# Experts in program order on TensorE, last w2 loads ahead of the norm loads, modulation rows spread by matmul, and pool places released tile by tile

## Chip, cores and metric

The kernel runs on one core of a Trainium2 chip (one TensorE, VectorE, ScalarE, GpSimd and SyncE with their own instruction queues, and 16 DMA engines). The metric is the device time of one execution in microseconds; the median of three runs counts.

## What is computed

One transformer block on 512 latent rows of 1024 channels, with 256 context rows beside them. Token mixing (latent attention and differential attention, gated, then one output projection) ends in a first norm; a mixture of 16 experts follows, of which each takes the 64 rows that score highest for it. The change lies in the second half, which is this, cut from the reference:

```python
y = gates[..., :D] * (o_mla @ w_o_mla) + gates[..., D:] * (o_diff @ w_o_diff)   # gated merge
o_lat = y @ w_out
x = layer_norm(ALPHA * x + g1 * o_lat, ln1_g, ln1_b)
h = x * (1.0 + sc2) + sh2
aff = softmax(h @ w_router + b_router)            # 16 experts
g, idx = lax.top_k(swapaxes(aff, 1, 2), 64)       # 64 rows per expert
xe = h[bidx, idx]
hid = silu(xe @ w1) * (xe @ w3)
ye = (hid @ w2) * g
x = layer_norm(ALPHA * x + g2 * zeros.at[bidx, idx].add(ye), ln2_g, ln2_b)
```

g1, sh2, sc2 and g2 are rows of 1024 modulation values, made out of c early in the kernel. Each expert's w1, w3 and w2 are 1024 x 1024 float32 (4 MB each, 201 MB in all), and each is read once.

## The kernel before

The program is written for a layer that records instructions, gives each tile a place in a pool, draws the waits, and lets a scheduler choose the order on each engine from modelled costs; the order is fixed when the program is built, and each engine then works through its own list. A pool that is opened on bytes of closed pools waits, as written, for every user of those pools.

**Merge, output projection, router.** For each of eight channel blocks of the latent branch (tile `om`, helper lines 82 to 84: a float32 product out of three passes of 128x512) VectorE gates it (line 902), GpSimd adds the other branch (line 904, `ys`), and ScalarE and VectorE split it into `yh`, `yl`. The gates are one tile `th` of 16 slices. The output projection (tile `po`) runs over two column halves of four token tiles, 24 matmuls each. g1 scales its result: in the first half afterwards (line 1007), in the second half beforehand, by multiplying the raw weights `outraw` on GpSimd (line 888), which are then split into `woh` and `wol` on ScalarE and VectorE (lines 75 and 78). For this g1 is needed on all 128 partitions (`g1b`); GpSimd's partition_broadcast makes it out of the row tile `rm` (line 968), and likewise `g2b` later (line 1187). After each `po` tile come four transposes, the router's products and, in the second half, the norm and the affinities; VectorE then finds the 64 largest.

**Experts in pairs.** For each of eight pairs: `gather` picks the rows by one-hot matmuls (line 1102, 32 matmuls of 128x128, into PSUM tiles `mx`; VectorE writes `xe`), `up_` does w1 and w3 of one expert (line 1140, `h`, 32 matmuls on 64 array columns each, two side by side), `back` transposes the one-hots (line 1120), `hid_t` transposes the hidden rows (line 1151), `down` does w2 (line 1159, `y`), and `scatter` scales, splits (`ye`) and puts the rows back: per column half four `mx` tiles of two matmuls (line 1171), each added to the accumulators by VectorE (line 1172). The last pair's `down` goes by three column parts (384, 384, 256 wide, line 1265), each put back while the next is computed (lines 1240 to 1254); then comes the second norm.

**Loads.** SyncE's queue issues nearly all of them in order (lines 934 and 936 for the experts). A load of 512 KB (384 KB in the first two parts of the last pair) fills one of 36 ring places of four pools, or one of nine places of tiles that are needed later (`places`: `gb`, `ye`, `acc0` to `acc3`, `hid`, `ohT`, `hidT`). A load waits until its place's last reader is done. A piece of weights is loaded when the program first asks for it, or earlier when `prefetch` is called. The gains and biases of the last norm (line 1222, `ln`) go into the places of `xe` and `hid`, which the last pair's `up_` and `hid_t` read, and are written ahead of the code that asks for most of the last w2 pieces.

Of the kernel before, what the change touches and what calls it, by code (L numbers as in the profile page):

```python
# [10 lines left out]
F32 = mybir.dt.float32  # L11
# [41 lines left out]
def _layer(tc, A, out, opened):  # L53
# [32 lines left out]
    # ---------------------------------------------------------------- constants and small vectors  # L86
# [12 lines left out]
    ghv = cp.tile([128, KD], F32, name="ghv")       # routed input = ghv * normed + bhv  # L99
# [21 lines left out]
    # ---------------------------------------------------------------- modulated input, first projection  # L121
# [10 lines left out]
    dqs = [rB.tile([128, NT, 256], F32, name="dq", tag="dq", bufs=2) for _ in range(2)]      # two heads each  # L132
# [92 lines left out]
    def mod_mul(q):  # L225
        """scale and shift of 256 channels, as rows"""
# [21 lines left out]
    def x_chunk(k, ci):  # L248
        """128 channels of the latent (0) or context (1) rows: transposed, modulated, split"""
# [16 lines left out]
    for q in range(4):  # L266
        # beside the products of these channels: what makes the next
# [15 lines left out]
    # rotary tables: cos, signed sin for the keys; the query ones carry the score scale  # L283
# [42 lines left out]
    one32 = mw.tile([128, 32], F32, name="one32")  # L326
    V.memset(one32, 1.0)
# [20 lines left out]
    def mod_sum(j, wa):  # L348
# [3 lines left out]
        for g in (2 * h, 2 * h + 1):  # L352
            T.matmul(pm[32 * g:32 * g + 32, :], one32, wa[:, (g % 2) * 512:(g % 2) * 512 + 512], start=True, stop=True)
# [3 lines left out]
    def chunk(col, n, cuts, evac, at, nxt):  # L357
        """projected columns; after the tiles in `at`, a part of the modulation's rows"""
# [27 lines left out]
    # latent query and key ranks: rms norm, transpose, gain  # L386
# [55 lines left out]
    def gates(g4, at=()):  # L442
        """a quarter of the gates, transposed: weights stationary"""
# [10 lines left out]
        for j in range(4):  # L454
            S.activation(th[:, g4 * 4 + j, :], ac[j], AF.Tanh, scale=0.5)
# [40 lines left out]
    # score tiles are emitted one by one; between them goes the product work of the tiles before  # L496
# [13 lines left out]
    def fill(parts):  # L510
        """one score tile is out: emit one of `parts` equal shares of the waiting work"""
# [12 lines left out]
    def flush(key=None):  # L524
        """emit all the waiting work, or what has `key`"""
# [7 lines left out]
    # transposed queries and keys: even heads of the differential attention, then the latent ones | odd heads  # L533
# [21 lines left out]
    def prep_t(hd, m, nm, src, c0, t0, nn):  # L555
# [8 lines left out]
        if nm == "q1":  # L564
            # the same with the halves of the contraction swapped
# [13 lines left out]
    def mod_end():  # L579
# [13 lines left out]
        # router columns with the norm's gain, less their mean: the norm's own mean then drops out  # L593
# [33 lines left out]
    # ---------------------------------------------------------------- differential attention  # L627
# [23 lines left out]
    def transposed(ws_, wt, j):  # L651
        """key chunks 2j, 2j+1 of two [128 q, 768] tiles, into [128 keys, 6, 256 q]"""
# [11 lines left out]
    def finish(hd, av, z0, key):  # L664
# [5 lines left out]
        def norm():  # L670
# [3 lines left out]
            # rows are scaled by the first map's sum: so is the guard under the root  # L674
# [23 lines left out]
    def key_rows():  # L698
        """the rotated key part, on rows 64-96 of every head's keys"""
# [35 lines left out]
    for hd in range(DH):  # L735
# [3 lines left out]
        for half in range(2):  # L739
# [6 lines left out]
            for t in (2 * half, 2 * half + 1):  # L746
# [9 lines left out]
                # sum0 * (softmax0 - lam * softmax1) = e0 + e1 * (-lam * sum0 / sum1)  # L756
# [24 lines left out]
    # ---------------------------------------------------------------- latent attention  # L781
# [16 lines left out]
    def diff_out(c, hl, jj):  # L798
# [4 lines left out]
        V.scalar_tensor_tensor(th[:, KD + j, :], th[:, KD + j, :], 1.0, ps, op0=OP.add, op1=OP.mult)  # L803

    for h in range(HEADS):
# [4 lines left out]
        for half in range(2):  # L810
# [52 lines left out]
    # ---------------------------------------------------------------- gated merge  # L863
# [14 lines left out]
    def w_out_load(hf, kk, page_):  # L878
        """two contraction chunks of a column half of w_out"""
# [15 lines left out]
    for c in range(4):  # L895
        hl = wos[c]
        for jj in range(2):
# [4 lines left out]
            V.scalar_tensor_tensor(g, th[:, j, :], 1.0, ps, op0=OP.add, op1=OP.mult)  # L902
            ys = yt.tile([128, 512], F32, name="ys")
            G.tensor_tensor(ys, g, th[:, KD + j, :], op=OP.add)
# [6 lines left out]
    # ---------------------------------------------------------------- expert weights: pages filled ahead  # L911
# [426 lines left out]
```

## Time and profile before

| what | value |
|---|---|
| runs | 1096.82, 1097.37, 1098.73 us (median 1097.37) |
| span of the profiled execution | 1094.2 us, first to last instruction |
| median of the runs less that span | 3.2 us |
| TensorE busy | 1007.4 us (92%) |
| weight loads on TensorE | 630.1 us |
| VectorE, ScalarE, GpSimd busy | 454.8, 276.0, 204.4 us |
| mean granted TensorE clock | 0.976 |
| DMA | 266.97 MB, mean 244 GB/s |

The profiled execution is known by its span alone; the runs' times have 3.2 us around it. In the profile PE is TensorE's matmuls, PEld its weight loads, DVE VectorE, ACT ScalarE, POOL GpSimd, SPq SyncE's queue of transfers. A float32 matmul appears as two records (so 4 records of `h` are one 512 KB page of weights), a float32r pass as one. The ends of matmuls are modelled and records overlap, so that a group's time over its count says more than the length of one. "idle before <- X" is what ended the wait.

### The profile page before, as it was taken

The page shows a single profiled execution, that of the slowest core. Times are in us where ns is not written, and L with a number is a line of the kernel's source. Part 1 is how long each engine was busy: PE and PEld are TensorE (multiplying, and loading weights), DVE is VectorE, ACT ScalarE, POOL GpSimd, SP SyncE. Part 2 cuts the span into 40 slices and gives each one's busy share as a digit, 9 for nine tenths or more (in the row PEclk, how much of TensorE's full clock was granted, in tenths as well). Part 3 has the DMA queues.
Part 4 walks back from the last instruction along what each step waited for, and adds up shares of the span by engine and source line. Part 5 has one row for each costly group of instructions (what it writes and reads, how often), then busy time and mean ns, then how long its engine had stood idle before and what let it go on. Part 6 is the DMA issues. An engine that isn't in the chain of part 4 may idle for free.

```text
span 1094.2 us, 13748 instructions
## 1 busy us (share of the span) xinstructions
PE 1007.4 (92%) x5259; PEld 630.1 (58%) x5259; DVE 454.8 (42%) x832; ACT 276.0 (25%) x551; POOL 204.4 (19%) x193
## 2 busy tenths in 40 slices
PE   6999998998899999997849999999999999999972
PEld 5888977677787777675536634444434434343331
DVE  2372377643677466463584221303022131303127
ACT  1222325244677455431210101010101010100001
POOL 2340022021675222143214200000000000000004
PEclk9999999999899999999889999999999999999997
DMA  9943357741002000176678999999999999999082
GB/s 302 288 154 106 97 169 247 243 140 39 20 20 74 20 20 21 39 269 235 245 270 304 404 329 411 409 409 409 409 409 409 409 410 408 409 410 400 14 283 97
DMA packets 101209, 266.97 MB, mean 244 GB/s; under 512 B 14020, under 2 KB 37528, under 8 KB 101144
## 3 DMA queue, kind: packets, MB, share of 16 engines
q1 hardware_dynamic: 100248, 264.52, 65.8%
q0 software_dynamic: 320, 1.05, 0.3%
q8 instruction: 41, 0.67, 0.3%
q10 hardware_dynamic: 576, 0.52, 0.1%
q14 instruction: 24, 0.20, 0.1%
HBM read 261.47 MB, written 2.10 MB: 241 GB/s over the span
## 4 chain that ended last, share of the span: by engine, by line
PE 75%; DVE 9%; DMA 5%; ACT 4%; issue 3%; POOL 2%; SPq 0%; DVEq 0%; ACTq 0%; POOLq 0%
PE h L1140 22%; PE y L1159 9%; PE mx L1102 6%; PE acc L84 4%; PE acc L83 4%; PE sc L648 4%; PE acc L82 4%; PE mx L1171 3%; PE tpb L656 3%; PE av L836 2%; DMA wa<-w_ada 2%; DMA wraw<-w_in 2%; PE y L1265 1%; PE av L772 1%; PE tp L232 1%
## 5 line engine op out<-in xcount | busy, mean ns | idle before, releaser
L1140 PE MATMUL h<-wr,xe 128*64 128x512 f32 x1024 | 250.0, 601 | 0.0
L1140 PEld LDWEIGHTS h<-wr,xe 128*64 128x64 f32 x1024 | 76.0, 136 | 110.4 <-issue 94.5
L1159 PE MATMUL y<-wr,hidT 128*64 128x512 f32 x448 | 99.6, 595 | 0.7 <-ACT hidT L1152 0.7
L1146 DVE TENSOR_TENSOR hid<-hid,h 128x512 f32<-128x512 f32 x16 | 11.0, 687 | 203.6 <-PE h L1140 203.6
L1102 PEld LDWEIGHTS mx<-oh,xn 128*128 128x128 f32 x512 | 62.7, 195 | 39.9 <-issue 38.7
L637 DVE TENSOR_REDUCE nm<-sc 128x1 f32<-128x768 f32 x64 | 61.0, 954 | 38.7 <-PE sc L648 38.2
L1115 POOL TENSOR_TENSOR oh<-oh,aff 128x512 f32<-128x512 f32 x8 | 8.4, 1049 | 361.9 <-PE mx L1102 353.1
L1102 PE MATMUL mx<-oh,xn 128*128 128x128 f32 x512 | 72.6, 289 | 1.7 <-DVE oh L1094 1.7
L1159 PEld LDWEIGHTS y<-wr,hidT 128*64 128x64 f32 x448 | 34.0, 137 | 57.8 <-issue 53.2
L638 ACT ACTIVATE P<-sc,nm 128x768 f32<-128x768 f32 x64 | 57.6, 900 | 35.0 <-DVE nm L637 26.0
L1145 ACT ACTIVATE hid<-h 128x512 f32<-128x512 f32 x16 | 9.6, 597 | 195.1 <-PE h L1140 195.1
L75 ACT ACTIVATE whi<-wraw 128x1024 fp32r<-128x1024 f32 (+1 forms) x32 | 33.5, 1046 | 99.6 <-DMA wraw<-w_in 80.9
L78 DVE TENSOR_TENSOR wlo<-wraw,whi 128x1024 fp32r<-128x1024 f32 (+1 forms) x32 | 38.7, 1211 | 43.9 <-PE acc L83 28.7
L82 PE MATMUL acc<-xlh,whi 128*128 128x512 f32 x128 | 51.0, 398 | 3.6 <-ACT whi L75 2.2
L82 PE MATMUL acc<-whi,xlh 128*128 128x512 f32 (+1 forms) x128 | 49.5, 391 | 1.0 <-ACT whi L75 1.0
L83 PE MATMUL acc<-xll,whi 128*128 128x512 f32 x128 | 50.0, 391 | 0.0
L84 PE MATMUL acc<-xlh,wlo 128*128 128x512 f32 x128 | 49.4, 394 | 0.3 <-DVE wlo L78 0.3
L84 PE MATMUL acc<-whi,xll 128*128 128x512 f32 (+1 forms) x128 | 48.8, 382 | 0.5 <-POOL xll L78 0.5
L83 PE MATMUL acc<-wlo,xlh 128*128 128x512 f32 (+1 forms) x128 | 48.8, 381 | 0.2 <-DVE wlo L78 0.2
L1172 DVE TENSOR_TENSOR acc<-acc,mx 128x512 f32<-128x512 f32 x56 | 36.0, 684 | 30.0 <-PE mx L1171 30.0
L648 PE MATMUL sc<-K,Q 96*128 96x512 f32 (+1 forms) x192 | 43.9, 355 | 1.3 <-ACT P L638 1.0
L820 POOL TENSOR_SCALAR P<-P,zm 128x768 f32<-128x768 f32 x32 | 30.0, 940 | 80.0 <-DVE zm L819 75.1
(333 smaller groups left out, 1691.4 us busy)
## 6 DMA issues: line engine op xcount, KB each, us to landing
wr<-moe_w SPq DMA_DIRECT2D x372, 512.0 KB, 10.2
wa<-w_ada SPq DMA_DIRECT2D x32, 512.0 KB, 4.0
wraw<-w_in SPq DMA_DIRECT2D x28, 512.0 KB, 4.7
wa<-w_ada SPq DMA_DIRECT2D x8, 1024.0 KB, 9.7
wr<-moe_w SPq DMA_DIRECT2D x16, 384.0 KB, 8.1
outraw<-w_out SPq DMA_DIRECT2D x8, 512.0 KB, 9.6
xq<-x SPq DMA_DIRECT2D x4, 512.0 KB, 7.9
q<-q SPq DMA_DIRECT2D x16, 128.0 KB, 2.3
```

The costliest lines, as they stand in the source:

```text
L75: S.activation(hi, src, AF.Copy)
L78: (eng_lo or V).tensor_tensor(lo, src, f(hi), op=OP.subtract)
L82: T.matmul(ps, lh, rh, start=start, stop=False)
L83: T.matmul(ps, lh, rl, start=False, stop=False)
L84: T.matmul(ps, ll, rh, start=False, stop=stop)
L637: V.tensor_reduce(nm, ps[:, :768], axis=AX.X, op=OP.max, negate=True)
L638: S.activation(p, ps[:, :768], AF.Exp, bias=nm, accum_out=z)
L648: T.matmul(ps[:, a:b], l, r[:, a:b], start=i == 0, stop=i == len(passes) - 1)
L1102: T.matmul(ps[:, kk * 128:(kk + 1) * 128], xn[t][:, k * 128:(k + 1) * 128], o[:, t].rearrange("p e s -> p (e s)"), start=t == 0, stop=t == ...
L1140: T.matmul(ph[i][64 * hf:64 * hf + 64, :], xe[:, k, sl], w[:, hf * 512:(hf + 1) * 512], start=k == 0, stop=k == KD - 1)
L1159: T.matmul(py[hf][r0:r0 + 64, :], hT[:, e % 2, fc % 4, fc // 4, :], w[:, hf * 512:(hf + 1) * 512], start=fc == 0, stop=fc == KD - 1)
L1172: V.tensor_tensor(acc[t][:, hs], acc[t][:, hs], ps, op=OP.add)
```

## The change

1. Every pool is opened with `reuse_waits="tile"`: a tile waits only for the earlier users of its own bytes. `th` becomes 16 tiles.
2. `spread` takes the place of partition_broadcast for `g1b` and `g2b`: a matmul of a row of ones with the row of `rm` into PSUM, and a copy by ScalarE.
3. From the first `gather` to the last matmul TensorE issues in the order in which the program is written (`manual_schedule`), and that is rewritten: `scatter` of a pair comes in the middle and at the end of the next pair's first `up_`, in blocks of eight matmuls; `gather` is not broken up; both `down` follow each other.
4. All remaining loads are asked for (`prefetch(len(order_r))`) ahead of the two `ln` loads.

```diff
-        kw = dict(name=name, bufs=bufs)
+        kw = dict(name=name, bufs=bufs, reuse_waits="tile")
...
+    def spread(dst, i, p, ps):
+        T.matmul(ps, one2[p:p + 1, 0:1].to_broadcast([1, 128]), rm[i][p:p + 1, :], start=True, stop=True)
+        S.activation(dst, ps, AF.Copy)
...
-    th = rT.tile([128, 2 * KD, SEQ], F32, name="th")
+    th_ = [rT.tile([128, SEQ], F32, name=f"th{j}") for j in range(2 * KD)]
+    th = [th_[2 * (j % KD) + j // KD] for j in range(2 * KD)]
...
-        G.partition_broadcast(g1b[:, g * 512:(g + 1) * 512], rm[0][32 * g:32 * g + 1])
+        spread(g1b[:, g * 512:(g + 1) * 512], 0, 32 * g, psc.tile([128, 512], F32, name="om", bufs=4))
...
-            G.partition_broadcast(g2b[:, g * 512:(g + 1) * 512], rm[1][64 + 32 * g:65 + 32 * g])
+            spread(g2b[:, g * 512:(g + 1) * 512], 1, 64 + 32 * g, psd.tile([128, 512], F32, name="mx", bufs=3))
...
+    order_.enter_context(tc.manual_schedule(engines={mybir.EngineType.PE}))
+    xe, o, steps = gather(0)
+    run(steps[:4])
+    waiting = None
+    for pr in range(E_N // 2):
+        last = pr == E_N // 2 - 1
+        hid = me.tile([128, 2, 512], F32, name="hid")
+        if waiting:
+            s0 = scatter(*waiting, 0)
+            up_(2 * pr, xe, hid, lambda: run(s0))
+            run(scatter(*waiting, 1))
+            ohT, gt = back(pr, o)
+        else:
+            up_(2 * pr, xe, hid, lambda: run(steps[4:]))
         up_(2 * pr + 1, xe, hid)
+        if not waiting:
+            ohT, gt = back(pr, o)
         hT = me.tile([128, 2, 4, 2, CAP], F32, name="hidT")
         hid_t(hid, hT, 0)
+        if last:
+            hid_t(hid, hT, 1)
+            break
+        xe, o, steps = gather(pr + 1)
+        run(steps)
+        hid_t(hid, hT, 1)
         if pr == 0:
             g2b = base()
+        py = [psd.tile([128, 512], F32, name="y", bufs=2) for _ in range(2)]
+        for i in range(2):
+            down(2 * pr + i, hT, py)
+        waiting = py, ohT, gt
...
+    prefetch(len(order_r))
     ln2 = []
```

**TensorE, end of a middle pair.** These rows are TensorE's list around the end of one of the middle pairs (`h` is up_, `y` down, `mx<-oh,xn` gather, `mx<-ident,hid` hid_t, `mx<-ye,ohT` scatter, `mx<-ident,oh` back; xN counts matmuls), before:

```order
L1140 MATMUL h<-wr,xe 64x512 x2
L1102 MATMUL mx<-oh,xn_4485 128x128
L1102 MATMUL mx<-oh,xn_4486 128x128
L1102 MATMUL mx<-oh,xn_4487 128x128
L1140 MATMUL h<-wr,xe 64x512 x10
L1159 MATMUL y<-wr,hidT 64x512 x2
L1151 MATMUL mx<-ident,hid 128x128 x4
L1159 MATMUL y<-wr,hidT 64x512 x30
L1171 MATMUL mx<-ye,ohT 128x512 x3
L1140 MATMUL h<-wr,xe 64x512
L1171 MATMUL mx<-ye,ohT 128x512 x3
L1140 MATMUL h<-wr,xe 64x512 x2
```

and at the same place in the changed program:

```order
L1109 MATMUL mx<-oh,xn_4498 128x128
L1109 MATMUL mx<-oh,xn_4499 128x128
L1109 MATMUL mx<-oh,xn_4500 128x128
L1154 MATMUL mx<-ident,hid 128x128 x4
L1162 MATMUL y<-wr,hidT 64x512 x32
L1146 MATMUL h<-wr,xe 64x512 x16
L1175 MATMUL mx<-ye,ohT 128x512 x8
L1146 MATMUL h<-wr,xe 64x512 x16
L1175 MATMUL mx<-ye,ohT 128x512 x8
L1126 MATMUL mx<-ident,oh 128x128 x4
L1146 MATMUL h<-wr,xe 64x512 x32
L1154 MATMUL mx<-ident,hid 128x128 x4
```

Before, gather and scatter go three matmuls at a time between ones and twos of up_; now each is one block, and a pair has six places where 64-column and 128-column matmuls meet.

**SyncE, end of the list.** The last loads before (`wr` weights, `ln` the last norm's rows; 362 full pages, then the column parts):

```order
L936 DMA wr<-moe_w 128x1024 x362
L934 DMA wr<-moe_w 128x2x384 x3
L1222 DMA ln_7468<-ln_g 128x1024
L1222 DMA ln_7470<-ln_b 128x1024
L934 DMA wr<-moe_w 128x2x384 x13
L934 DMA wr<-moe_w 128x4x256 x4
L1293 DMA out<-acc 128x768 x3
```

and now:

```order
L941 DMA wr<-moe_w 128x1024 x362
L939 DMA wr<-moe_w 128x2x384 x16
L939 DMA wr<-moe_w 128x4x256 x4
L1237 DMA ln_7531<-ln_g 128x1024
L1237 DMA ln_7533<-ln_b 128x1024
L1309 DMA out<-acc 128x768 x3
```

Seventeen weight loads, which stood behind the two `ln` loads, stand ahead of them.

**GpSimd, merge to router.** GpSimd's list around `g1b` before (ISA rows are the broadcast and what surrounds it):

```order
L904 TENSOR_TENSOR ys<-gy,th 128x512 x8
L968 ISA
L968 ISA g1b<-rm 128x512 x2
L888 ISA
L888 TENSOR_TENSOR outraw<-outraw,g1b 128x1024 x4
L119 TENSOR_TENSOR mv<-mv,negh 128x1
```

and now:

```order
L909 TENSOR_TENSOR ys<-gy,th_707 128x512
L909 TENSOR_TENSOR ys<-gy,th_709 128x512
L893 TENSOR_TENSOR outraw<-outraw,g1b 128x1024 x4
L124 TENSOR_TENSOR mv<-mv,negh 128x1
L1049 TENSOR_SCALAR xn_4497<-xn_4497,mv 128x1024
```

The products with `g1b` follow the sums at once; the two matmuls of `spread` stand on TensorE between the last `om` and the first `po`, ScalarE's two copies behind its last `yh`. On VectorE two of the four `wol` splits of the second half now stand ahead of the first `r<-po,g1b`, and one behind each of the next two instructions.

## Rows read from the trace of the kernel before

**Rows 1.** The page: span, and the GB/s of 40 equal slices.
```profile
span 1094.2 us, 13748 instructions
...
GB/s 302 288 154 106 97 169 247 243 140 39 20 20 74 20 20 21 39 269 235 245 270 304 404 329 411 409 409 409 409 409 409 409 410 408 409 410 400 14 283 97
```

**Rows 2.** Windows: stretch, us, busy of PE, PEld, DVE, ACT, POOL, clock, DMA share, GB/s.
```profile
525.00:530.00 5.00, 5.00 (x22) 3.44 (x21) 2.56 (x5) 0.88 (x2) 0.00 (x0) 0.54 0.90 303
...
700.00:800.00 100.00, 98.54 (x480) 42.72 (x482) 19.82 (x36) 10.15 (x21) 2.10 (x2) 1.00 1.03 409
...
1016.00:1020.00 4.00, 4.00 (x22) 1.39 (x20) 0.24 (x1) 0.00 (x0) 0.00 (x0) 1.00 0.00 0
```

**Rows 3.** Waits of SyncE's queue, 1000 to 1070 us: total, times, longest.
```profile
SPq L1222 <- PE h L1140: 36.0, 1, 36.0
```

**Rows 4.** Timeline of SyncE's queue at the end: start, us, what.
```profile
1045.06 16.62 SPq L934 DMA_DIRECT2D wr<-moe_w  x17
```

**Rows 5.** Chain that ended last, order of time: start, us; whole run.
```profile
629.00 6.88 PE y L1159 x32
...
989.73 13.08 PE y L1159 x60
```

**Rows 6.** The chain in its last 60 us.
```profile
1073.74 0.50 DVE y L1240
```

**Rows 7.** Timeline of TensorE, output projection.
```profile
494.04 0.50 PE L82 MATMUL po<-woh,yh 128*128 128x512 f32 x1 [1.53 <-ACT yh L905]
...
524.39 1.11 PE L1011 MATMUL om<-ident,xn 128*128 128x128 f32 x4 [9.06 <-DVE xn L1008]
```

**Rows 8.** The chain in the same stretch, single matmuls.
```profile
526.36 0.43 PE po L83
...
529.77 0.24 PE po L82
```

**Rows 9.** Timeline of GpSimd and the instructions of line 968 around it.
```profile
L968 POOLq MODIFY_POOL_CONFIG  x2: 14/14/14, 494.5 to 494.5; - x2
...
500.24 1.48 POOL L968 PARTITION_BROADCAST g1b<-rm  x2 [5.69 <-issue]
512.51 11.28 POOL L888 TENSOR_TENSOR outraw<-outraw,g1b 128x1024 f32<-128x1024 f32 x4 [10.79 <-issue]
```

**Rows 10.** Timeline of VectorE beside those products and after them.
```profile
516.03 5.55 DVE L78 TENSOR_TENSOR wol<-outraw,woh 128x1024 fp32r<-128x1024 f32 x2 [3.83 <-ACT woh L75]
...
524.26 1.21 DVE L78 TENSOR_TENSOR wol<-outraw,woh 128x1024 fp32r<-128x1024 f32 x1
```

**Rows 11.** Timeline of TensorE, second pair.
```profile
647.25 23.39 PE L1140 MATMUL h<-wr,xe 128*64 128x512 f32 x106
...
679.71 6.74 PE L1102 MATMUL mx<-oh,xn 128*128 128x128 f32 x58
686.29 0.60 PE L1151 MATMUL mx<-ident,hid 128*128 128x128 f32 x4
```

**Rows 12.** Timeline of TensorE, fifth pair.
```profile
842.11 1.08 PE L1140 MATMUL h<-wr,xe 128*64 128x512 f32 x4
843.12 0.94 PE L1102 MATMUL mx<-oh,xn 128*128 128x128 f32 x6
843.98 1.08 PE L1140 MATMUL h<-wr,xe 128*64 128x512 f32 x4
...
864.93 13.10 PE L1159 MATMUL y<-wr,hidT 128*64 128x512 f32 x60
```

**Rows 13.** Timeline of TensorE, last pair's down by column parts.
```profile
1050.69 6.42 PE L1265 MATMUL y<-wr,hidT 128*64 128x384 f32 x24 [4.03 <-DMA wr<-moe_w]
...
1062.46 4.08 PE L1265 MATMUL y<-wr,hidT 128*64 128x384 f32 x24
...
1071.75 1.95 PE L1265 MATMUL y<-wr,hidT 128*64 128x256 f32 x16
```

**Rows 14.** The page's groups: busy us, mean ns, idle before.
```profile
L1172 DVE TENSOR_TENSOR acc<-acc,mx 128x512 f32<-128x512 f32 x56 | 36.0, 684 | 30.0 <-PE mx L1171 30.0
```

More of the change, by code (lines that the diff above doesn't have):

```diff
@@ L352, in mod_sum @@
         for g in (2 * h, 2 * h + 1):
-            T.matmul(pm[32 * g:32 * g + 32, :], one32, wa[:, (g % 2) * 512:(g % 2) * 512 + 512], start=True, stop=True)
+            T.matmul(pm[32 * g:32 * g + 32, :], one2[:, 0:1].to_broadcast([128, 32]), wa[:, (g % 2) * 512:(g % 2) * 512 + 512], start=True, stop=True)
             dma(bm[32 * g:32 * g + 32, :512], b_ada[4 + 4 * i + g:5 + 4 * i + g].to_broadcast([32, 512]))
@@ L802, in diff_out @@
         wo_mul(ps, hl, jj, oD)
-        V.scalar_tensor_tensor(th[:, KD + j, :], th[:, KD + j, :], 1.0, ps, op0=OP.add, op1=OP.mult)
+        V.scalar_tensor_tensor(th[KD + j], th[KD + j], 1.0, ps, op0=OP.add, op1=OP.mult)
     for h in range(HEADS):
@@ L901, in _layer @@
             g = yt.tile([128, 512], F32, name="gy")
-            V.scalar_tensor_tensor(g, th[:, j, :], 1.0, ps, op0=OP.add, op1=OP.mult)
+            V.scalar_tensor_tensor(g, th[j], 1.0, ps, op0=OP.add, op1=OP.mult)
             ys = yt.tile([128, 512], F32, name="ys")
-            G.tensor_tensor(ys, g, th[:, KD + j, :], op=OP.add)
+            G.tensor_tensor(ys, g, th[KD + j], op=OP.add)
             S.activation(yh[:, j, :], ys, AF.Copy, scale=0.5)
@@ L1087, in _layer, with gather @@
     acc = [place(f"acc{t}").tile([128, D], F32, name="acc", tag=f"acc{t}", bufs=1) for t in range(NT)]
-    def gather(pr, between=None):
+    def gather(pr):
         e0 = 2 * pr
@@ L1096, in gather, with eighth @@
         xe = me.tile([128, KD, 128], F32, name="xe")
-        for hf in range(2):
-            ps = psd.tile([128, 512], F32, name="mx", bufs=3)
-            for kk in range(4):
-                k = 4 * hf + kk
-                for t in range(NT):
-                    T.matmul(ps[:, kk * 128:(kk + 1) * 128], xn[t][:, k * 128:(k + 1) * 128],
-                             o[:, t].rearrange("p e s -> p (e s)"), start=t == 0, stop=t == NT - 1)
-            for kk in range(4):
-                k = 4 * hf + kk
-                V.tensor_scalar(xe[:, k, :], ps[:, kk * 128:(kk + 1) * 128], ghv[:, k:k + 1], bhv[:, k:k + 1],
-                                op0=OP.mult, op1=OP.add)
-            if between:
-                between(xe, hf)
-        return xe, o
+        pss = {}
+        def eighth(k):
+            hf, kk = divmod(k, 4)
+            if kk == 0:
+                pss[hf] = psd.tile([128, 512], F32, name="mx", bufs=3)
+            for t in range(NT):
+                T.matmul(pss[hf][:, kk * 128:(kk + 1) * 128], xn[t][:, k * 128:(k + 1) * 128],
+                         o[:, t].rearrange("p e s -> p (e s)"), start=t == 0, stop=t == NT - 1)
+            if kk == 3:
+                for i in range(4):
+                    j = 4 * hf + i
+                    V.tensor_scalar(xe[:, j, :], pss[hf][:, i * 128:(i + 1) * 128], ghv[:, j:j + 1], bhv[:, j:j + 1],
+                                    op0=OP.mult, op1=OP.add)
+        return xe, o, [lambda k=k: eighth(k) for k in range(KD)]
     def back(pr, o):
@@ L1128, in back, with up_ @@
         return ohT, gt
-    def up_(e, xe, hid, half=None):
+    def up_(e, xe, hid, between=None):
         sl = slice((e % 2) * CAP, (e % 2) * CAP + CAP)
-        if half == 1:
-            ph = first[0]
-        else:
-            ph = [psd.tile([128, 512], F32, name="h", bufs=3) for _ in range(2)]
-        for k in range(KD) if half is None else range(4 * half, 4 * half + 4):
+        ph = [psd.tile([128, 512], F32, name="h", bufs=3) for _ in range(2)]
+        for k in range(KD):
+            if k == KD // 2 and between:
+                between()
             for i, n in enumerate(("w1", "w3")):
@@ L1141, in up_ @@
                              start=k == 0, stop=k == KD - 1)
-        if half == 0:
-            first.append(ph)
-            return
         S.activation(hid[:, e % 2, :], ph[0], AF.Silu)
@@ L1160, in down, with scatter, tile_ @@
                          start=fc == 0, stop=fc == KD - 1)
-    def scatter(py, ohT, gt, g2b):
-        for hf in range(2):
-            hs = slice(hf * 512, (hf + 1) * 512)
-            ye = me.tile([128, 2, 512], F32R, name="ye")
-            V.scalar_tensor_tensor(py[hf], py[hf], gt[:, hf:hf + 1], g2b[:, hs], op0=OP.mult, op1=OP.mult)
-            split(ye[:, 0, :], ye[:, 1, :], py[hf])
-            for t in range(NT):
-                ps = psd.tile([128, 512], F32, name="mx", bufs=3)
-                for i in range(2):
-                    T.matmul(ps, ohT[:, hf, t * 128:(t + 1) * 128], ye[:, i, :], start=i == 0, stop=i == 1)
-                V.tensor_tensor(acc[t][:, hs], acc[t][:, hs], ps, op=OP.add)
+    def scatter(py, ohT, gt, hf):
+        hs = slice(hf * 512, (hf + 1) * 512)
+        ye = me.tile([128, 2, 512], F32R, name="ye")
+        V.scalar_tensor_tensor(py[hf], py[hf], gt[:, hf:hf + 1], g2b[:, hs], op0=OP.mult, op1=OP.mult)
+        split(ye[:, 0, :], ye[:, 1, :], py[hf])
+        def tile_(t):
+            ps = psd.tile([128, 512], F32, name="mx", bufs=3)
+            for i in range(2):
+                T.matmul(ps, ohT[:, hf, t * 128:(t + 1) * 128], ye[:, i, :], start=i == 0, stop=i == 1)
+            V.tensor_tensor(acc[t][:, hs], acc[t][:, hs], ps, op=OP.add)
+        return [lambda t=t: tile_(t) for t in range(NT)]
     def base():
@@ L1186, in base, with run @@
         for g in range(2):
-            G.partition_broadcast(g2b[:, g * 512:(g + 1) * 512], rm[1][64 + 32 * g:65 + 32 * g])
+            spread(g2b[:, g * 512:(g + 1) * 512], 1, 64 + 32 * g, psd.tile([128, 512], F32, name="mx", bufs=3))
         return g2b
-    first = []
-    hid = me.tile([128, 2, 512], F32, name="hid")
-    g_next = gather(0, lambda xe, hf: up_(0, xe, hid, hf))
-    for pr in range(E_N // 2 - 1):
-        xe, o = g_next
-        if pr:
-            hid = me.tile([128, 2, 512], F32, name="hid")
-            up_(2 * pr, xe, hid)
+    def run(steps):
+        for fn in steps:
+            fn()
+    order_ = ExitStack()
+    order_.enter_context(tc.manual_schedule(engines={mybir.EngineType.PE}))
[12 more added lines that the diff above has]
+            up_(2 * pr, xe, hid, lambda: run(steps[4:]))
         up_(2 * pr + 1, xe, hid)
-        ohT, gt = back(pr, o)
+        if not waiting:
+            ohT, gt = back(pr, o)
         hT = me.tile([128, 2, 4, 2, CAP], F32, name="hidT")
-        py = [psd.tile([128, 512], F32, name="y", bufs=2) for _ in range(2)]
         hid_t(hid, hT, 0)
-        down(2 * pr, hT, py)
-        g_next = gather(pr + 1)
+        if last:
[4 more added lines that the diff above has]
+        hid_t(hid, hT, 1)
         if pr == 0:
             g2b = base()
-        hid_t(hid, hT, 1)
-        down(2 * pr + 1, hT, py)
-        scatter(py, ohT, gt, g2b)
-    xe, o = g_next
-    ohT, gt = back(E_N // 2 - 1, o)
-    hid = me.tile([128, 2, 512], F32, name="hid")
-    hT = me.tile([128, 2, 4, 2, CAP], F32, name="hidT")
-    for i in range(2):
-        up_(E_N - 2 + i, xe, hid)
-        hid_t(hid, hT, i)
+        py = [psd.tile([128, 512], F32, name="y", bufs=2) for _ in range(2)]
+        for i in range(2):
+            down(2 * pr + i, hT, py)
+        waiting = py, ohT, gt
+    prefetch(len(order_r))
     ln2 = []
@@ L1271, in _layer @@
     rest()
+    order_.close()
     ov = out[0].rearrange("(t p) d -> p t d", p=128)
```

4 lines of the change are left out of this document (1 added, 3 removed).

## The prediction

> **What bounds the kernel now.** I read the page first, for the span and the GB/s of its slices [rows 1]. From the twenty-first slice on the expert weights stream, at 409 GB/s, until a slice near the end falls to 14. Next, the windows [rows 2]: between 700 and 800 us TensorE is busy 98.54 of 100 us at clock 1.00, while the DMA share is 1.03. A pair's 48 pages of 0.524 MB take 61.5 us at 409 GB/s, so both are full. Which of them ends last? The waits of TensorE there name no transfer, and ring places and early places keep up to 45 pages loaded ahead. So TensorE's own list bounds the middle of the run. The chain of waits gives the length of that list: its last y of the first pair ends at 629.00 + 6.88 = 635.88 and that of the seventh at 989.73 + 13.08 = 1002.81 [rows 5], six periods in 366.9 us, 61.2 each.
>
> Two other places matter. At the end of the stream the DMA moves 0 GB/s from 1016 to 1020 [rows 2]. The queue's waits say why: the two norm loads wait 36.0 us for the last up_ [rows 3], and 17 weight loads stand behind them, issued from 1045.06 on [rows 4]. TensorE then waits 4.03 us for such a page, and runs 24 records in 6.42 us where the later 24 take 4.08 [rows 13]. And in the output projection TensorE is idle 9.06 us for VectorE's `xn` [rows 7], and matmuls of 0.24 us take 0.43 behind it [rows 8], in a window whose clock is 0.54 [rows 2], near the lower of the two levels.
>
> **Part by part.** The sum is made against the profiled span of 1094.2 us; the median of the runs stands 3.2 us above it, and I add that at the end.
>
> *Broadcast to spread, first use.* The 9.06 us come about thus. GpSimd changes its configuration at 494.5, the broadcasts start at 500.24 after 5.69 us of "issue", and its products start at 512.51 after another 10.79 [rows 9]. Until then no `wol` can be split, and the two VectorE splits beside the products take 5.55 us, against 1.21 for one alone [rows 10]. With the broadcast gone the products can start at about 496 and end near 508, ahead of the 515.3 at which TensorE began to wait. I count off 9.06 and the low clock behind it: eleven matmuls by 0.43 − 0.24 us, 2.1. I add the spread. A record of `h` takes 23.39 / 106 = 0.2207 us [rows 11]; two records of each of two 64-column halves make a full-width float32 matmul 0.88, two of them 1.8. They stand where TensorE waited 1.53 us for `yh` [rows 7]; I leave 0.6 of them exposed. What is late next is VectorE, which has the splits ahead of its first result; I allow 1.0. Together **−9.6** (bounds: 0, if another wait takes its place, and −12, if none does).
>
> GpSimd's products now fall beside VectorE's split of the merge and its `wol`. The rows show the price of that company: 2.78 us for a split beside the products, 1.21 alone [rows 10]. The Trainium skill, "SBUF — State Buffer", section "Who interferes with whom", says that VectorE and GpSimd share a port pair under an exclusive lock, so that one blocks the other. By the rows' longer splits four of them cost 6.3 us more on VectorE, most of it ahead of the first `po`; by the lock the products too would stretch, and TensorE could wait again. That is a rival below.
>
> *Spread, second use.* Two more full-width matmuls inside the first pair, with nothing on TensorE to hide them: 2 × 0.88 = **+1.8**. The broadcast that they replace was off TensorE's path (bounds 0 and 3.6, should the copies hold a place of `mx`).
>
> *Program order in the six middle periods.* A pair now has 128 records of up_ at 0.2207 (28.2), 64 of down at 13.10 / 60 = 0.218 (14.0, [rows 12]), 64 of gather at 6.74 / 58 = 0.116 (7.4) and twelve transposes at 0.60 / 4 = 0.15 (1.8, [rows 11]), and 16 scatter matmuls at 0.24 (3.8, [rows 8]). That is 55.2. What does an interleaved order cost? Between 842.11 and 843.98 four records of `h` and six of gather take 1.87 us [rows 12], where the durations above make 1.58: 0.15 for each of two changes of shape. Six changes are left, 0.9: 56.1. Hand-overs are new. A scatter block has four `mx` tiles in three places, so that the fourth can wait for an accumulator add of 0.684 us [rows 14]; I take one such add per block, 1.4. The period is then 57.5, and six save 366.9 − 345.0 = **−21.9**. Bounds: 56.1 with nothing exposed; 59.9 with two waits of 1.53, as for `yh` [rows 7], and one add. I stay near the lower end because VectorE is busy under 20 of 100 us there [rows 2].
>
> *Last pair and loads.* From 1002.81 to the last scaling of y on VectorE at 1073.74 [rows 6] it took 70.9. Now up_, scatter and transposes take a pair less its gather and down, 57.5 − 14.0 − 7.4 = 36.1; four 256-wide full-width matmuls for the last part's accumulators 4 × 0.44 = 1.8; the parts at 4.08 / 24 and 1.95 / 16 a record 5.4 + 5.4 + 3.9 = 14.7 [rows 13]; two blocks of eight 384-wide scatter matmuls between them 8 × 0.18 each, with one add and two changes of shape, 4.9; VectorE's backlog ahead of the scaling 0.9. That is 58.4: **−12.5**. The cover is that the loads arrive. The 17 loads are 7.21 MB, 17.6 us at 409 GB/s [rows 2]; begun by 1016, where the rows show nothing moving, they end by 1034, and at about 1024 with the stream 9.6 us earlier. TensorE's last y would end near 1031. If the cover is gone, TensorE waits for pages as before, at most until the loads end. Each period of 57.5 against 61.5 of loads uses up 4 us of lead, some 24 of the 57.6 us that 45 pages are.
>
> *Rest.* The epilogue behind 1073.74 is 20.5 us and not changed. The norm loads now come last, are ready long before it, and hold nothing up. Tile-wise release leaves the order of the stages ahead of the merge as it was; where it ends a wait early, another engine's wait follows there. I count 0 (bounds −3 and +1).
>
> Sum: −9.6 + 1.8 − 21.9 − 12.5 = −42.2, a span of 1052.0, and a time of **1055 us** (own range 1049 to 1061).
>
> **Rivals.**
> *The loads become the bound.* For it: the DMA share is 1.03 already [rows 2], and TensorE is to need pages faster than they come. Against it: 45 pages of lead. If the stream does not move up, it ends at 1034; with 2.8 us of TensorE behind the last page, 20.5 and 3.2 that is about **1060**, and 1063 with the last part at the lower clock.
>
> *The router's wait stays.* By the lock above, and with VectorE's splits ahead of `r`, TensorE waits as long as before; all 9.6 are lost: **1065**. For it: 5.55 us for two splits [rows 10]. Against it: the products start 16 us earlier.
>
> *The hand-overs are exposed.* 59.9 and not 57.5 in seven periods is 17 us: **1072**. For it: with no up_ between the blocks every wait of gather on `xe` or of scatter on `ye` stands bare on TensorE. Against it: the blocks stand half an up_ behind what they need.
>
> *Slower.* Bare hand-overs put the clock to its lower level each time. The price of one is a wait of 1.53 [rows 7] and 6.42 − 4.08 = 2.34 [rows 13], 3.9. The point from which it decides is 42.2 / 7 = 6.0 a pair: with one the kernel is still faster, with two it loses 7 × 7.8 = 54, **1109**. For it: low clock behind the waits of 4.03 and 9.06. Against it: no hand-over is forecast to be near these. The Trainium skill, "TensorE: Matmul & The Clock Gate", section "HAM oscillation — how this bites in real kernels", describes the same with waits for DMA between groups of matmuls, each of which puts the clock back; the row of 4.03 us agrees, the stretch at clock 1.00 shows none.
>
> *The change does nothing.* TensorE's list is fixed by the program, so it does what the order shows; only if 409 GB/s bound the periods all along would most of it be lost, and then loads would be named in TensorE's waits.
>
> **How the numbers follow.** Forecast 0.61, loads 0.15, router 0.10, hand-overs 0.10, slower 0.02, nothing 0.02. The low end takes the better bounds of the merge (−2.4) and most of a period of 56.1 (up to −9.8): 1046. The high end takes in the loads, the router and hand-overs: 1072; beyond it lie parts of the last and the two small cases. A measurement of this kernel tells 0.2% (2.2 us) from no change; only the last two cases are not faster by that: 0.96, 0.02, 0.02.
>
> **What would show it.** TensorE's row ahead of the first transpose of `xn` with an idle time under 2 us, and no configuration change on GpSimd; ends of y 57 to 58 us apart, with clock 1.00; 409 GB/s into the slice before last of the stream and no 0 in it; no wait on `wr` in the last parts; 20 to 21 us behind the last scaling of y. Periods of 60 or more without waits on loads would make the fourth part wrong, waits on `wr` the fifth, an idle time of some 9 us at the router the first.

## The result, and the profile after

The changed kernel takes 1061.34 us in the median of four runs against 1097.09 of the kernel before; the ratio is 0.9673, with an interval of 0.9656 to 0.9689. The forecast was 1055 us. Its whole range, 1046 to 1072, holds the result; the own range of the forecast case, 1049 to 1061, ends just under it. Of the kernel with both edits (under Experiments), one execution took 2510.97 us, more than twice any other, and is left out. The stages tell another story than the total. The times below run from the end of one row of TensorE to the end of the next; the last scaling of y is VectorE's row (1039.7 us in the changed kernel), and the epilogue runs from it to the end of the span.

| stretch | before | forecast | after |
|---|---|---|---|
| start to the last y of the first pair | 635.9 | 628.1 | 635.9 |
| six periods, to the last y of the seventh pair | 366.9 | 345.0 | 339.0 |
| last pair, to the last scaling of y | 70.9 | 58.4 | 64.8 |
| epilogue | 20.5 | 20.5 | 20.5 |
| span | 1094.2 | 1052.0 | 1060.2 |

Three of the four stretches are off, by +7.8, -6.0 and +6.4 us, and the middle one hides 6.0 of the other 14.2. The page of the changed kernel, where [rows 1] stood:

```profile
span 1060.2 us, 13786 instructions
...
PE 981.3 (93%) x5267; PEld 617.0 (58%) x5267; DVE 451.9 (43%) x831; ACT 277.9 (26%) x555; POOL 201.5 (19%) x189
...
GB/s 296 310 145 117 91 142 238 239 185 61 29 32 65 31 20 2 20 138 273 272 203 306 337 302 409 409 409 409 409 409 409 409 409 409 409 409 408 409 373 119
```

The hole of 14 GB/s is gone: 409 GB/s run into the third slice from the end. TensorE's timeline, at the down blocks of the first, second, fifth, sixth and seventh pair, and three rows of the last pair's second up_ (start, us, and in brackets the idle time before):

```profile
621.98 13.95 PE L1162 MATMUL y<-wr,hidT 128*64 128x512 f32 x64
...
676.75 13.96 PE L1162 MATMUL y<-wr,hidT 128*64 128x512 f32 x64
...
841.10 13.95 PE L1162 MATMUL y<-wr,hidT 128*64 128x512 f32 x64
...
899.60 13.95 PE L1162 MATMUL y<-wr,hidT 128*64 128x512 f32 x64
...
961.00 13.95 PE L1162 MATMUL y<-wr,hidT 128*64 128x512 f32 x64
...
1009.41 1.08 PE L1146 MATMUL h<-wr,xe 128*64 128x512 f32 x4 [0.20 <-DMA wr<-moe_w]
1010.70 1.08 PE L1146 MATMUL h<-wr,xe 128*64 128x512 f32 x4 [0.21 <-DMA wr<-moe_w]
1011.96 1.08 PE L1146 MATMUL h<-wr,xe 128*64 128x512 f32 x4 [0.18 <-DMA wr<-moe_w]
```

Four periods take (841.10 - 621.98) / 4 = 54.8 us, then come 58.5 and 61.4. In the end a page of up_, four records, takes 1.28 us and waits for its load each time: 0.524 MB in 1.28 us are 409 GB/s. The chain of waits says from where on the loads decide (start, us, what):

```profile
841.17 13.88 PE y L1162 x64
855.05 4.21 PE h L1146 x19
859.26 10.18 DMA wr<-moe_w
869.50 10.63 DMA wr<-moe_w
880.20 10.18 DMA wr<-moe_w
...
1023.75 9.21 DMA wr<-moe_w
1033.01 1.94 PE y L1280 x14
```

From the second pair's up_ (635.9 us) to 859 us the chain runs through TensorE's list alone; from 855 to 1040 us 70% of it are loads. So the order was made faster than the stream that feeds it, and from there on the stream set the pace.

The router is as it was, answering to [rows 7, 9, 10]. GpSimd's products, then VectorE, then TensorE, each by its timeline:

```profile
495.88 11.30 POOL L893 TENSOR_TENSOR outraw<-outraw,g1b 128x1024 f32<-128x1024 f32 x4 [1.71 <-ACT g1b L119]
```

```profile
499.40 5.57 DVE L78 TENSOR_TENSOR wol<-outraw,woh 128x1024 fp32r<-128x1024 f32 x2 [3.85 <-ACT woh L75]
504.90 0.68 DVE L1012 TENSOR_TENSOR r<-po,g1b 128x512 f32<-128x512 f32 x1
505.50 2.76 DVE L78 TENSOR_TENSOR wol<-outraw,woh 128x1024 fp32r<-128x1024 f32 x1
508.18 0.68 DVE L1013 SCALAR_TENSOR_TENSOR xn<-xn,r 128x512 f32<-128x512 f32 x1
```

```profile
508.92 1.11 PE L1016 MATMUL om<-ident,xn 128*128 128x128 f32 x4 [9.37 <-DVE xn L1013]
```

The products start 16.6 us earlier and TensorE still idles 9.37 us. Three splits now stand ahead of the first `xn`, and TensorE meets them with no transpose done, where before it had two token tiles' behind it (TensorE's timeline, before):

```profile
502.80 0.60 PE L1011 MATMUL om<-ident,xn 128*128 128x128 f32 x4
...
505.86 0.60 PE L1011 MATMUL om<-ident,xn 128*128 128x128 f32 x4
```

### The profile page after: what moved, and what is told of

Same layout as the page of the kernel before. It is cut to its first block, busy times and chain, and to the rows that moved or that the text cites. A ratio compares the mean times of both kernels' runs of the same rounds, so it can differ in the third digit from the quotient of the medians.

```text
span 1060.2 us, 13786 instructions
## 1 busy us (share of the span) xinstructions
PE 981.3 (93%) x5267; PEld 617.0 (58%) x5267; DVE 451.9 (43%) x831; ACT 277.9 (26%) x555; POOL 201.5 (19%) x189
## 4 chain that ended last, share of the span: by engine, by line
PE 66%; DMA 17%; DVE 8%; POOL 3%; issue 3%; ACT 2%; SPq 0%; POOLq 0%; DVEq 0%; ACTq 0%
PE h L1146 14%; DMA wr<-moe_w 12%; PE y L1162 9%; PE mx L1109 6%; PE acc L84 5%; PE acc L83 5%; PE acc L82 5%; PE sc L653 4%; DMA wa<-w_ada 4%; PE tpb L661 3%; PE av L841 2%; PE mx L1175 2%; PE tp L237 1%; PE av L777 1%; DVE wol L78 1%
## 5 line engine op out<-in xcount | busy, mean ns | idle before, releaser
L1146 PE MATMUL h<-wr,xe 128*64 128x512 f32 x1024 | 233.8, 598 | 8.8 <-DMA wr<-moe_w 7.1
L1146 PEld LDWEIGHTS h<-wr,xe 128*64 128x64 f32 x1024 | 68.2, 137 | 163.1 <-issue 106.5
L1162 PEld LDWEIGHTS y<-wr,hidT 128*64 128x64 f32 x448 | 31.5, 137 | 61.8 <-issue 57.9
L643 ACT ACTIVATE P<-sc,nm 128x768 f32<-128x768 f32 x64 | 57.6, 900 | 31.9 <-DVE nm L642 22.9
L1109 PE MATMUL mx<-oh,xn 128*128 128x128 f32 x512 | 61.4, 283 | 1.4 <-DVE oh L1099 1.4
L1109 PEld LDWEIGHTS mx<-oh,xn 128*128 128x128 f32 x512 | 60.3, 199 | 2.5 <-issue 2.1
L75 ACT ACTIVATE ye<-y 128x512 fp32r<-128x512 f32 (+2 forms) x17 | 9.7, 572 | 178.6 <-DVE y L1169 98.7
L1169 DVE SCALAR_TENSOR_TENSOR y<-y,gate,g2b 128x512 f32<-128x512 f32 x14 | 9.9, 754 | 92.6 <-PE y L1162 92.6
## 6 DMA issues: line engine op xcount, KB each, us to landing
wr<-moe_w SPq DMA_DIRECT2D x372, 512.0 KB, 10.2
outraw<-w_out SPq DMA_DIRECT2D x8, 512.0 KB, 10.2
```

Source lines behind the costliest of these rows:

```text
L643: S.activation(p, ps[:, :768], AF.Exp, bias=nm, accum_out=z)
L1109: T.matmul(pss[hf][:, kk * 128:(kk + 1) * 128], xn[t][:, k * 128:(k + 1) * 128], o[:, t].rearrange("p e s -> p (e s)"), start=t == 0, stop ...
L1146: T.matmul(ph[i][64 * hf:64 * hf + 64, :], xe[:, k, sl], w[:, hf * 512:(hf + 1) * 512], start=k == 0, stop=k == KD - 1)
L1162: T.matmul(py[hf][r0:r0 + 64, :], hT[:, e % 2, fc % 4, fc // 4, :], w[:, hf * 512:(hf + 1) * 512], start=fc == 0, stop=fc == KD - 1)
```

## Experiments

Theory S: from about 859 us on the stream of loads sets the end; how much earlier it ends depends on when TensorE frees the first ring places, and a faster list later is worth nothing. Theory T is the forecast: TensorE's list sets the end. Ratios are to the kernel before, with 95% intervals; a difference between two ratios is given in microseconds of 1097.1.

**Without the order.** The expert stage of before (its gather, up_, scatter, the loop and the tail), the other three parts of the change kept:

```diff
-    order_.enter_context(tc.manual_schedule(engines={mybir.EngineType.PE}))
...
+    first = []
+    hid = me.tile([128, 2, 512], F32, name="hid")
+    g_next = gather(0, lambda xe, hf: up_(0, xe, hid, hf))
...
```

> The changed kernel with the expert stage in the order of before; spread, tile-wise release and the early weight loads stay. Theory S (the stream of loads sets the end of the changed kernel from about 859 us on, and how early TensorE frees the first ring places): the old list takes 61.2 us a pair against 61.4 of loads, so TensorE is the later one again all through, the last scaling comes about 10 us before the one of before because the stream does not stop, and the time is 1080 to 1088 us. Theory T (the forecast: TensorE's list sets the end in both): the order was worth 21.9 us and its part of the last pair, 1085 to 1092. Rival R (loads bound both kernels all along, so the order is worth nothing): 1061 to 1064.

1090.64 us, ratio 0.9929 (0.9905 to 0.9953): 28 us are given back. The time lies in T's range and 2.6 us above S's. TensorE waits for no page there, and SyncE's queue (waits, 980 to 1070 us) is ahead and stands:

```profile
SPq L1228 <- PE h L1145: 14.7, 1, 14.7
```

The rival that loads bound both kernels falls. The size fits T and misses S, so this run does not favour S.

**Without the early prefetch.**

```diff
-    prefetch(len(order_r))
     ln2 = []
```

> The changed kernel with the two norm loads again ahead of the last 17 weight loads. Theory S: with the loads as the bound the queue comes to the norm loads only about when the last up_ ends, so the stop is short: the restart, and 1 MB of norm rows ahead of the weights, 4 to 7 us, 1064 to 1069 us, and TensorE waits for the pages behind them. Theory T: the queue is far ahead, comes to them some 15 us before the last up_ ends, and stands: 12 us or more, 1073 or above.

1068.44 us, 0.9724 (0.9694 to 0.9755): 5.6 us, as S said and under half of T's 12 or more. The queue's wait of [rows 3], 36.0 us, is now 7.1, and TensorE's wait behind it (timeline) is

```profile
1023.41 6.17 PE L1279 MATMUL y<-wr,hidT 128*64 128x384 f32 x24 [3.83 <-DMA wr<-moe_w]
```

**With partition_broadcast for both rows.**

```diff
-        spread(g1b[:, g * 512:(g + 1) * 512], 0, 32 * g, psc.tile([128, 512], F32, name="om", bufs=4))
+        G.partition_broadcast(g1b[:, g * 512:(g + 1) * 512], rm[0][32 * g:32 * g + 1])
...
-            spread(g2b[:, g * 512:(g + 1) * 512], 1, 64 + 32 * g, psd.tile([128, 512], F32, name="mx", bufs=3))
+            G.partition_broadcast(g2b[:, g * 512:(g + 1) * 512], rm[1][64 + 32 * g:65 + 32 * g])
```

> The changed kernel with GpSimd's partition_broadcast for both rows in place of the two spreads. Theory S: only the time of the first up_ counts, which moved by some 2 us between the two kernels: 1060 to 1065 us, whatever the idle time at the router is. Theory T (first term of the forecast): 9.6 - 1.8 us are given back, 1067 to 1071.

1060.22 us, 0.9652 (0.9616 to 0.9688): no difference that these runs can tell. S said so, T's 1067 to 1071 falls. TensorE's timeline has the pattern of before, two token tiles' transposes and then the wait:

```profile
503.87 0.66 PE L1016 MATMUL om<-ident,xn 128*128 128x128 f32 x4 [0.95 <-DVE xn L1013]
...
507.01 0.60 PE L1016 MATMUL om<-ident,xn 128*128 128x128 f32 x4
...
525.14 1.11 PE L1016 MATMUL om<-ident,xn 128*128 128x128 f32 x4 [8.69 <-DVE xn L1013]
```

The wait of about 9 us stands at 516 to 525 or at 500 to 509, with more or less done ahead of it. What the two spreads bring and cost nearly cancels: with the broadcasts the first gather starts at 574.26 and not 572.15, 2.1 us later, and from there to the last y of the first pair it takes 62.3 us and not 63.8.

**With pool-wise waits.**

```diff
-        kw = dict(name=name, bufs=bufs, reuse_waits="tile")
+        kw = dict(name=name, bufs=bufs)
```

> The changed kernel with pools that wait for all users of the closed pools, as before; the order of every engine stays the same. Both theories: the waits ahead of the merge come back, at most some 3 us, 1060 to 1065 us; by S the first up_ starts later by the same amount as the time is longer, by T the early loads alone are later and the time stays.

1066.60 us, 0.9700 (0.9662 to 0.9739): 1.6 us above what both theories said and 3 us more in the ratio, but the intervals overlap. In its trace the wait of TensorE for `oM` ahead of the merge is back, 1.4 us, the first transpose of `xn` starts at 512.39 and not 508.92, and the first gather at 576.30 and not 572.15. That the start of the experts moves with the time is what S said; the size stays open.

**Loads a third fewer.** From the second pair on, w3's product reads w1's page.

```diff
-             for k in range(KD) for n in ns]
+             for k in range(KD) for n in ns if pr == 0 or n != "w3"]
...
-                w = piece(e, n, k)
+                w = w if i and e >= 2 else piece(e, n, k)
```

> The changed kernel in which, from the second pair on, w3's product reads the page of w1: w3's 112 pages are not loaded, so the output of 14 experts is another, and the loads are a third fewer while TensorE's list and every tile stay as they are. Theory S (loads set the end): without them TensorE keeps its period of 54.8 us to the end, the last y of the seventh pair ends at 635.9 + 6 x 54.8 = 965, the last scaling comes near 1020, and the time is 1039 to 1045 us; no wait on a weights page is left. Rival H (TensorE slows down by itself after some pairs, by hand-overs or its clock): 1055 us or more.

1043.29 us in one run, as S said. TensorE waits for no page, and the chain runs through its list to the last pair's down (start, us, what):

```profile
910.25 6.87 PE h L1146 x32
917.12 2.19 PE mx L1175 x8
919.30 7.02 PE h L1146 x32
926.32 2.19 PE mx L1175 x8
929.09 13.88 PE h L1146 x64
943.57 7.15 PE mx L1109 x64
951.15 13.88 PE y L1162 x64
965.03 6.87 PE h L1146 x32
```

965.03 - 910.25 = 54.8 in the seventh pair too, where the changed kernel took 61.4. TensorE does not slow down by itself; a third of the loads less takes some 18 us off the changed kernel, a single run against a median.

**More work on TensorE.** Two gathers, of the fourth and fifth pair, are computed twice.

```diff
+        if pr in (2, 3):
+            pd = psd.tile([128, 512], F32, name="mx", bufs=3)
...
```

> The changed kernel in which two gathers (of the fourth and fifth pair) are computed a second time into a place that nobody reads, 32 matmuls or some 7.2 us more on TensorE in each, 14.4 together. Theory S: TensorE's list alone would end at 1043 + 14 = 1057 us, ahead of the loads, so the waits on pages begin later and are 14 us fewer, and the time stays, 1060 to 1063 us. Theory T (TensorE's list sets the end): 1074 to 1077 us.

1063.24 us, 0.9684 (0.9649 to 0.9718): 1.2 us more, within the interval and at the upper end of S's range, for 14.3 us more of matmuls. T's 1074 to 1077 falls. The chain shows where they went: the loads take over at 997 and not at 859 us.

```profile
988.40 7.03 PE h L1146 x32
995.43 1.50 PE mx L1175 x6
996.93 10.18 DMA wr<-moe_w
```

**Ring places sooner.** In the first pair gather goes behind both downs, and with it the second spread, which `base` holds.

```diff
-        xe, o, steps = gather(pr + 1)
-        run(steps)
-        hid_t(hid, hT, 1)
-        if pr == 0:
-            g2b = base()
+        if pr:
+            xe, o, steps = gather(pr + 1)
+            run(steps)
+            hid_t(hid, hT, 1)
...
+            if pr == 0 and i == 0:
+                hid_t(hid, hT, 1)
+        if pr == 0:
+            xe, o, steps = gather(pr + 1)
+            run(steps)
+            g2b = base()
```

> The changed kernel with the gather of the second pair behind both downs of the first, so that TensorE frees the 16 w2 pages some 8 us sooner; the amount of work on TensorE is the same. Theory S: the queue's wait of 11.5 us for a y shrinks by 6 to 8 us, the last page lands as much earlier, 1053 to 1056 us. Theory T (TensorE's list): the same list in another order, with one more bare hand-over of rows: 1061 to 1063 us.

1056.80 us, 0.9616 (0.9587 to 0.9645): 6.3 us faster than the changed kernel with the same work on TensorE, and 0.8 us above S's range. In its trace TensorE comes to the second pair's up_ later, 65.0 us after the first gather and not 63.6, so its list did not bring the gain. The queue's waits between 605 and 636 us, of the changed kernel and then of this one (in total, times, longest):

```profile
SPq L941 <- PE y L1162: 17.1, 13, 11.5
```

```profile
SPq L941 <- PE y L1162: 4.6, 7, 2.3
```

The longest wait is 9.2 us shorter, where S had said 6 to 8: the 7.4 us of gather and the 1.9 of the spread together come to 9.3.

**g1 behind both halves.** GpSimd's products go, and g1 scales the result in the second half as in the first.

```diff
-        if hf:
-            G.tensor_tensor(wraw[hf, kk], wraw[hf, kk], g1b[:, None, 512:].to_broadcast([128, 2, 512]), op=OP.mult)
...
-            r = ps
-            if hf == 0:
-                r = mp.tile([128, 512], F32, name="r", bufs=2)
-                V.tensor_tensor(r, ps, g1b[:, hs], op=OP.mult)
+            r = mp.tile([128, 512], F32, name="r", bufs=2)
+            V.tensor_tensor(r, ps, g1b[:, hs], op=OP.mult)
```

> The changed kernel without GpSimd's products of the raw output weights: g1 scales the result in both column halves, so that the four splits wait for ScalarE alone. Theory S with the router explained by GpSimd's products (11.3 us) and the splits beside them (2.8 us each): the idle time of 9.4 us ahead of the first transpose falls under 3, four more VectorE products of 0.7 come in, of which the last is on the path, the first up_ starts 6 to 8 us earlier and the time is 1053 to 1056 us. Rival: VectorE's search for the largest values is what the experts wait for and does not move: 1060 to 1063 us.

1056.32 us, 0.9610 (0.9586 to 0.9635): 6.9 us faster than the changed kernel and 0.3 above S's range. The first gather starts at 564.78, 7.4 us earlier, as S said. The idle time did not fall under 3: splits still stand ahead of the first `r`, but they are short now. VectorE and TensorE, timelines:

```profile
494.45 3.50 DVE L78 TENSOR_TENSOR wol<-outraw,woh 128x1024 fp32r<-128x1024 f32 x3 [0.69 <-ACT woh L75]
```

```profile
499.33 1.11 PE L1012 MATMUL om<-ident,xn 128*128 128x128 f32 x4 [3.74 <-DVE xn L1009]
```

The rival, that the experts wait for VectorE's search for the largest values, which would not move, falls.

**Both edits,** in two sets of runs.

> Both edits together. Theory S: they act on the same thing, the time at which ring places come free, one by the start of the first up_ and one behind it, so they add: 1045 to 1049 us, with TensorE still waiting for pages in the last pairs. Theory T: only the first counts, 1053 to 1056 us.

1052.72 us in the median of the three executions kept, 0.9585 (0.9548 to 0.9623). S missed: it had said 1045 to 1049, which full addition would give. The time lies just under T's 1053 to 1056; against T's reason, that the moved gather is worth nothing, stand the 6.3 us that it brought alone.

> The kernel with both edits once more, in more rounds, since its three left open whether the edits add. Theory S: they act on the same thing one behind the other, so the ratio to before lies at 0.956 to 0.960, under the 0.961 of either edit alone. Rival: with the first the second is worth nothing, 0.960 to 0.963.

1051.92 us, 0.9574 (0.9544 to 0.9603): 10.9 us faster than the changed kernel, 13.2 being the sum of the two, and inside S's range for it. It has the lowest ratio of all versions that compute the same result and is clear of both kernels. That the edits add in part is likely; its interval still touches that of either alone, so by how much stays open.

**The parts alone, on the kernel before.** The early prefetch alone:

```diff
+    prefetch(len(order_r))
     ln2 = []
```

> The kernel before with one part of the change: all remaining weight loads ahead of the two norm loads. In before TensorE's list is the later one, the queue reaches the norm loads far ahead and stands for 36.0 us, and TensorE then loses 4.0 us of waiting and 2.3 us of lower clock. Theory S: those come back and no more, 1087 to 1091 us, since here the loads have 14 us or more to spare, as in the changed kernel without its order. Theory T (the forecast counted the whole of the last pair, 12.5 us, partly to the order): the same part of it, 1088 to 1092. Rival: the 17 loads were hidden anyway and the time stays at 1096 to 1099.

1090.84 us, 0.9933 (0.9909 to 0.9957): 7.4 us, as both theories said. The order alone, with the norm loads ahead of the last weights as before:

```diff
+    order_.enter_context(tc.manual_schedule(engines={mybir.EngineType.PE}))
+    xe, o, steps = gather(0)
...
```

> The kernel before with the new expert order alone; broadcast, pool-wise waits and the norm loads ahead of the last weights stay. Theory S: TensorE's periods fall to 54.8 us until the lead of loads is used up near 860 us, and the loads set the end; with 7 us for the norm loads and 5 for the pools, as their removal from the changed kernel cost, 1071 to 1076 us. Theory T: the order brings its 21.9 us and the norm loads cost the 12 us forecast, 1080 us or more.

1069.24 us, 0.9729 (0.9696 to 0.9762): 29.7 of the 35.9 us of the whole change, and 2 us better than S said. Its chain gives way to loads at 881.61 us. T's 1080 or more is far off.

## Why the prediction came out right, point by point

The number was inside the range, and what happened was the first rival, to which 0.15 had been given: "the stream does not move up, it ends at 1034", 1060 us. The last page landed at 1033.0. Two of the signs that the forecast had named against itself appeared, waits on `wr` in the last parts and some 9 us of idle time at the router. The forecast's own mechanism for the end was wrong.

- **The lead of the loads** is the step that failed: "Each period of 57.5 against 61.5 of loads uses up 4 us of lead, some 24 of the 57.6 us that 45 pages are". A period uses 61.4 - 54.8 = 6.6 us. And from the last y of the first pair, 635.9, to 859.3 are 4.08 periods, so the lead was some 27 us and not 57.6, an estimate from these rows. Why so short can be counted, though no run took it apart: nine of the 45 places belong to pieces that the first pair reads (the numbers 2 to 27 of `places`, of 48 pieces a pair), and a load takes 10.2 us from issue to landing in the page's list of DMA issues, so about eight pages are under way: 45 - 9 - 8 = 28 pages, 36 us at most. And the ring had stood full, with the queue waiting 11.5 us for a y just ahead.
- **The order** was forecast at -21.9 in six periods and brought -27.9, the first four at 54.8 us. The sum of bare durations, 55.2, was right; the 0.9 for changes of shape and the 1.4 for hand-overs were not there. TensorE's waits between 570 and 858 us name nothing in these periods; x_thin shows the same through the seventh pair. Had the loads kept up, it would have been 366.9 - 6 x 54.8 = 38, an estimate.
- **Broadcast to spread** was forecast at -9.6. The first gather started at 572.15 in place of 574.21, and u_bcast finds nothing. The step that failed is "the products can start at about 496 and end near 508, ahead of the 515.3 at which TensorE began to wait": they ran from 495.88 to 507.2, but TensorE began to wait at 508.92 - 9.37 = 499.6. The prediction held TensorE's arrival fixed while it moved the work of VectorE: TensorE now needs the first `xn` and not the third. The second rival, that the router's wait stays, came true beside the first; on its own it had been priced at 9.6 us. What the wait is made of was seen rightly: f_g1 takes the products away and gains 6.9. The splits took 2.8 us each beside them, and 1.17 without. The Trainium skill, "SBUF — State Buffer", section "Who interferes with whom", lets one of VectorE and GpSimd block the other. The rows agree in both directions: GpSimd's sums `ys` take 2.11 us beside two splits and 1.27 each with none (timelines of GpSimd and VectorE, changed kernel). The products took 11.28 us before and 11.30 now, beside splits both times, and no run shows them alone.

```profile
487.09 2.11 POOL L909 TENSOR_TENSOR ys<-gy,th 128x512 f32<-128x512 f32 x1 [2.43 <-DVE gy L907]
491.63 2.54 POOL L909 TENSOR_TENSOR ys<-gy,th 128x512 f32<-128x512 f32 x2 [2.43 <-DVE gy L907]
...
486.87 3.42 DVE L78 TENSOR_TENSOR wol<-outraw,woh 128x1024 fp32r<-128x1024 f32 x2
```

- **Spread, second use,** was forecast at +1.8. The row is 1.88 us long, on TensorE's path, and from the first gather to the last y of the pair it took 63.8 us, against 62.3 with the broadcasts in the same order (u_bcast) and 61.7 in the order of before. Right in size, and it falls on the releases of ring places.
- **The last pair** was forecast at -12.5 and brought -6.1. The work was sized well: in x_thin the stretch from the last y of the seventh pair to the epilogue is 1041.5 - 20.5 - 965.0 = 56.0 us, against 58.4 in the sum. The other 8.8 us are pages: "The cover is that the loads arrive." They come late, and those of the column parts also more slowly than the 409 GB/s reckoned (below).
- **The norm loads.** In the old order they cost 7.4 us (a_norm), in the new one 5.6 (u_norm), though the queue stands 36.0 us in the one and 7.1 in the other. In these two, the length of the queue's stall did not set its cost.
- **Tile-wise release** was counted at 0, with bounds of -3 and +1. u_pool lies 3.0 us above the changed kernel in the ratio, with intervals that overlap, so the term may have been worth its lower bound.
- **The epilogue** is 20.5 us, as said. **The slower rival,** clock drops at bare hand-overs, did not come: the clock is 1.00 from 630 to 1030 us, through the 0.2 us waits too.

The low error of the total is thus partly luck: +7.8 and +6.4 us against -6.0.

## What to carry to other kernels

When two resources are both full, making one of them faster pays only until the buffer between them is empty: work out the lead in time, from pages that are free and landed and not from places, and what each period takes from it, and forecast the time twice, by each resource, with the later end as the answer. Once the stream is the bound, only what starts it earlier or frees its places sooner counts, so look for the consumer's first pages and not its steady state. When an operation that another engine waits for is moved forward, re-time that engine's arrival too: here a wait of some 9 us kept its length and only changed its place.

## What the hardware showed that was not expected

The column-part pages come more slowly than full ones: the windows of the changed kernel's last loads (stretch, us, busy of PE, PEld, DVE, ACT, POOL, clock, DMA share, GB/s) show 372 GB/s at a DMA share above 1 with the 384-wide pages, where full pages make 409. The last two rows are lower still, but there the 256-wide pages and the two norm loads (issued at 1028.45 and 1030.19) are under way too. No run changes the pages' form alone, so the cause is open.

```profile
1020.00:1022.00 2.00, 2.00 (x14) 0.97 (x12) 0.00 (x0) 0.00 (x0) 0.00 (x0) 1.00 1.06 372
...
1028.00:1030.00 2.00, 2.00 (x14) 0.86 (x11) 2.00 (x9) 0.00 (x0) 0.00 (x0) 1.00 1.08 357
1030.00:1032.00 2.00, 1.92 (x12) 0.71 (x9) 0.50 (x2) 0.00 (x0) 0.00 (x0) 1.00 1.13 346
```

And TensorE's blocks of different shapes follow one another without a gap that the rows show when each is long: the interleaved records of [rows 12] had given 0.15 us a change of shape, while in x_thin's chain the block of eight at 917.12 begins where the row before it ends, and the next `h` at 919.30, 2.18 us later, where it ends.
